# Attention values as two scaled float16 parts, and matmul operands at equal addresses modulo 512

## The chip, the cores and the metric

The kernel runs on one core of one Trainium2 chip. The metric is the device time of one execution in microseconds (us). Three runs of the kernel before gave 2252.26 us as their median (2251.11 to 2253.65).

## The reference

One layer of an encoder over 2048 frames of width 1024, all in float32. Cut to what matters here:

```python
h = rmsnorm(x, mix_norm_g)
q, k, v, u, vg = split(h @ w_in)              # 5 blocks of 512 columns; heads of 64
a = band_attention(q, k, v, q_g, k_g, rel)    # 8 heads; each 64-frame chunk sees itself and 8 before
g = spatial_gating(u, vg, norm_g, w_s, b_s)
x = x + concat(rmsnorm(a), rmsnorm(g)) @ w_out
h = rmsnorm(x, ffn_norm_g)
gate, up = split(h @ w_ffn_in)                # 2 x 2816
x = x + (silu(gate) * up) @ w_ffn_out

# in band_attention, with the probabilities of one head:
p = softmax(q @ k.T * 64 ** -0.5 + bias)
out = p @ v
```

## The kernel before

Every large product is made from operands that are split in two: `hi` is the float32 number rounded to TensorE's float32r, `lo` the rest. `split` (L80) makes them with a cast on ScalarE (L81) and a subtraction on VectorE (L82); `mm3` (L84) then runs three matmuls into one PSUM bank, hi by hi (L85), hi by lo (L86) and lo by hi (L87). Matmuls of 128 rows by 512 columns of this kind make up most of the program.

The stages, in order of time:

- **Input projection.** Two halves (`hf`) of 8 frame tiles by five column blocks (`b`: u, vg, q, k, v). `project` runs 24 matmuls for a tile of 128 frames (stationary `xh`/`xl`, moving `wh`/`wl`), and the block's `unit_*` takes the PSUM bank `ps`. There are four such banks. The next block's weights are loaded and split by `load_w` (L256), called when a block is at its seventh tile. In the first half a scheduler sets the order on every engine; from the second half on TensorE follows the order of the code. The first four tiles' attention (`early`) is woven into the second half.
- `unit_v` (L393) scales `ps` by the frame's `rx` on ScalarE and writes it as three bfloat16 parts: cast (L397), subtract (L398), cast (L399), subtract (L400), then a DMA to `v_d`.
- **Attention** of tiles 4 to 15, 96 (tile, head) steps, with the output projection's matmuls (`po`) fed between them. In each step TensorE makes the scores `S` (L171), transposes five 128x128 blocks of probabilities `pr` against the identity `ident` (L195, L198) and multiplies (`values`, L206). The transposed probabilities are two float16 parts, `ph` (cast with `PSCALE` on ScalarE, L201) and `pl` (VectorE, L202). For each of the five key blocks `values` runs five matmuls of 64 columns, `ph` with the three parts of v and `pl` with two:

```python
seq = [(i, a, c) for i in range(nk) for a, cs in ((ph, 3), (pl, 2)) for c in range(cs)]
for n, (i, a, c) in enumerate(seq):
    nc.tensor.matmul(o, lhsT=a[:, i], rhs=vt[m + 1 - nk + i][:, c, h * HD : (h + 1) * HD], ...)
```

  The four early tiles have 1, 2, 3 and 4 key blocks and run the same code into `ev`; together that is 480 and 80 key blocks. `denominators` (L212) divides by the row sums.
- **First FFN product**, by a seven-product (Strassen) scheme: 44 blocks of 7 products of 12 matmuls (`bank`, stationary `wih`/`wil`, moving `yh`/`yl`), 3696 in all.
- **Second FFN product**, the same scheme: 7 products of 264 matmuls (`bank`, stationary `ah`/`al`, moving `oh`/`ol`), 1848 in all.

Tiles are placed by pools that grow from the left and from the right end of the on-chip memory. Small first tiles (`edge` on the right; the constants `ident`, `nhalf`, `g1`, `rx`, `identr` on the left) shift everything allocated after them, so an operand's address within a partition, taken modulo 512 bytes, follows from their sizes.

Of the kernel before, what the change touches and what calls it, by code (L numbers as in the profile page):

```python
# [8 lines left out]
F32 = mybir.dt.float32  # L9
F32R = mybir.dt.float32r  # L10
F16 = mybir.dt.float16
BF16 = mybir.dt.bfloat16
AF = mybir.ActivationFunctionType
ALU = mybir.AluOpType
AX = mybir.AxisListType
# [3 lines left out]
P = 128  # L19
SEQ = 2048  # L20
D = 1024
KT = D // P
NT = SEQ // P
H = 8
HD = 64
AW = H * HD
# [6 lines left out]
EPS = 1e-6  # L33
NEG = -1e30
PSCALE = 16384.0
NE = WIN - 1
EARLY = [(m, h) for h in range(H) for m in range(NE)]
LATE = [(m, h) for m in range(NE, NT) for h in range(H)]
# [4 lines left out]
def block_kernel(ctx: ExitStack, tc: tile.TileContext, x, xT, w_in, mixg, qg, kg, bias, sgug, wsT, bsp, outg, w_out, ffng, w_fi, w_fo, out):  # L43
    nc = tc.nc

    consts = ctx.enter_context(tc.tile_pool(name="consts", bufs=1))
    edge = ctx.enter_context(tc.tile_pool(name="edge", bufs=1, side="right"))
    edge.tile([P, 24], F32, name="edge")
    dram = ctx.enter_context(tc.tile_pool(name="dram", bufs=1, space=DRAM))

    kT_d = dram.tile([P, H, SEQ], F32, name="kT_d")
    qe_d = dram.tile([HD, H, NE, 2, P], F32, name="qe_d")
    qT_d = [qe_d[:, :, m] if m < NE else dram.tile([HD, H, 2, P], F32, name=f"qT_d{m}") for m in range(NT)]
    v_d = [dram.tile([P, 3, AW], BF16, name=f"v_d{m}") for m in range(NT)]
    g_d = [dram.tile([P, AW], F32, name=f"g_d{m}") for m in range(NT)]
    a_d = [dram.tile([P, AW], F32, name=f"a_d{m}") for m in range(NT)]
    y_d = [[[dram.tile([P, 512], F32, name=f"y_d{i}_{o}_{j}") for j in range(4)] for o in range(7)] for i in range(2)]
# [5 lines left out]
    nhalf = consts.tile([P, 8], F32, name="nhalf")  # L63
    nc.gpsimd.memset(nhalf, -0.5)

    g1 = consts.tile([P, KT], F32, name="g1")
    nc.scalar.dma_start(g1, mixg)
    rx = consts.tile([P, NT], F32, name="rx")

    def pool(stack, name, bufs, side="left", space=bass.MemoryType.SB):  # L70
        return stack.enter_context(tc.tile_pool(name=name, bufs=bufs, side=side if space != PSUM else None, space=space, reuse_waits="tile"))
# [8 lines left out]
    def split(hi, lo, src):  # L80
        nc.scalar.copy(hi, src)  # L81
        nc.vector.tensor_sub(lo, src, hi.bitcast(F32))  # L82
# [9 lines left out]
    apool = {}  # L92
    bt, vt, qd, kw, pvs, sums, xm, gn, an, mh, ml, heads = ({} for _ in range(12))
# [52 lines left out]
    def load_tile(m, q=True):  # L146
        if q:
            qd[m] = apool["qd"].tile([P, H, 2, P], F32R, tag="qd", name=f"qd{m}")
            nc.sync.dma_start(qd[m][:HD].bitcast(F32), qT_d[m])
            nc.sync.dma_start(qd[m][HD:].bitcast(F32), qT_d[m])  # L150
        vt[m] = apool["vt"].tile([P, 3, AW], BF16, tag="vt", name=f"vt{m}")
        nc.sync.dma_start(vt[m], v_d[m])

    def load_bias(h):
# [50 lines left out]
    def values(m, h, o):  # L205
        nk = min(m, WIN - 1) + 1  # L206
        ph, pl = heads.pop((m, h))
        seq = [(i, a, c) for i in range(nk) for a, cs in ((ph, 3), (pl, 2)) for c in range(cs)]
        for n, (i, a, c) in enumerate(seq):
            nc.tensor.matmul(o, lhsT=a[:, i], rhs=vt[m + 1 - nk + i][:, c, h * HD : (h + 1) * HD], start=n == 0, stop=n == len(seq) - 1)  # L210

    def denominators(pool, ss, k):  # L212
        rs = pool.tile([P, k], F32, tag="rs", name="rs")
        nc.vector.tensor_scalar_mul(rs, ss, PSCALE)
        nc.vector.reciprocal(rs, rs)
        return rs

# [18 lines left out]
    with ExitStack() as st:  # L236
        st1 = st.enter_context(ExitStack())
        tqk, raw = pool(st1, "tqk", 2), pool(st1, "raw1", 4)
        stg = st1.enter_context(ExitStack())
        big, c1 = pool(stg, "big1", 1), pool(stg, "c1", 1)  # L240
        sm, tmp, ws, xs = (pool(st, n, b, "right") for n, b in (("sm1", 4), ("tmp1", 2), ("ws", 4), ("xs", 4)))
        paux = pool(st, "paux", 4, space=PSUM)
# [10 lines left out]
                nc.vector.scalar_tensor_tensor(lo[:, j], r[:, j], s, hi[:, j].bitcast(F32), op0=ALU.mult, op1=ALU.subtract)  # L253
            return hi, lo

        def load_w(b, kp):  # L256
            r = raw.tile([P, 2, 512], F32, tag="raw", name=f"wr{b}_{kp}")
            hi = ws.tile([P, 2, 512], F32R, tag="wh", name=f"wh{b}_{kp}")
            lo = ws.tile([P, 2, 512], F32R, tag="wl", name=f"wl{b}_{kp}")
            nc.sync.dma_start(r, w_in[b, :, 2 * kp : 2 * kp + 2])  # L260
            split(hi, lo, r)
            return hi, lo

        def x_stats(t):
# [7 lines left out]
        def project(xt, w, tl, between=None):  # L272
            ps = pmm.tile([P, 512], F32, tag="mm", name="ps")
            c, o = divmod(tl, 4)
            s = slice(o * P, (o + 1) * P)
            for kt in range(KT):
                kp, j = divmod(kt, 2)
                xh, xl = xt[c][kp]
                wh, wl = w[kp]
                mm3(ps, xh[:, j, s], xl[:, j, s], wh[:, j], wl[:, j], kt == 0, kt == KT - 1)  # L280
                if between and kt in (1, 4, 7):
                    between()
            return ps
# [107 lines left out]
            later(3, fin)  # L391

        def unit_v(t, ps):  # L393
            e = tmp.tile([P, AW], F32, tag="f", name="ev", bufs=5)
            nc.scalar.activation(e, ps, AF.Copy, scale=rx[:, t : t + 1])
            vp = tmp.tile([P, 3, AW], BF16, tag="vp", name="vp")
            nc.scalar.copy(vp[:, 0], e)  # L397
            nc.vector.tensor_tensor(e, e, vp[:, 0], op=ALU.subtract)  # L398
            nc.scalar.copy(vp[:, 1], e)  # L399
            nc.vector.tensor_tensor(vp[:, 2], e, vp[:, 1], op=ALU.subtract)  # L400
            nc.sync.dma_start(v_d[t], vp)


        ep, eq, ek, eb, es, ev = ({} for _ in range(6))

        def open_early(stack):
            for n, bufs in (("in", 2), ("vt", 1), ("pr", 2), ("pp", 2), ("an", 1), ("sa", 4)):
                ep[n] = pool(stack, "e" + n, bufs)
            for m in range(NE):
                vt[m] = ep["vt"].tile([P, 3, AW], BF16, name=f"vte{m}")  # L410
                nc.sync.dma_start(vt[m], v_d[m])
            ep["a"] = ep["an"].tile([P, NE, H, HD], F32, name="a4")
            for h in range(2):
                early_in(h)
# [11 lines left out]
        def early(i):  # L426
            sp = dict(S=(paux, "aux"), T=(paux, "aux"), ap=ep, w=NE * P)
            if i < len(EARLY):
                m, h = EARLY[i]
                if m == 0:  # L430
                    es[h] = ep["sa"].tile([P, NE], F32, tag="es", name="es")
                scores(m, h, sp, eq[h][:, m], ek[h], eb[h], es[h][:, m : m + 1])
            if 1 <= i <= len(EARLY):
                m, h = EARLY[i - 1]
                flip(m, h, sp)
            if 2 <= i < len(EARLY) + 2:
                m, h = EARLY[i - 2]
                if m == 0:
                    ev[h] = paux.tile([P, NE, HD], F32, tag="aux", name="ev", padded_shape=[P, 8, HD])
                values(m, h, ev[h][:, m])  # L440
                if m == NE - 1:
                    rs = denominators(ep["sa"], es[h], NE)
                    nc.vector.tensor_tensor(ep["a"][:, :, h], ev[h], rs.unsqueeze(2).to_broadcast([P, NE, HD]), op=ALU.mult)
                    if h + 2 < H:
                        early_in(h + 2)
            if i == len(EARLY) + 2:
                for m in range(NE):
                    a = ep["a"][:, m].rearrange("p h d -> p (h d)")
                    att_scale(ep, a)
                    nc.sync.dma_start(a_d[m], a)  # L450
# [37 lines left out]
        for hf in range(2):  # L488
            for b, unit in enumerate(blocks):
                for tl in range(8):  # L490
                    t = hf * 8 + tl
                    if (hf, b, tl) == (1, 4, 2):
                        while due:
                            tick()
                        st1.close()
                        open_out(st_out)
                        mx["P"] = (paux, "aux")
                    if (hf, b) == (1, 4) and tl in (6, 7):
                        an[tl - 6] = None
                        mix_g(tl - 6)  # L500
                        mix_a(tl - 6)
                    if (hf, b, tl) == (1, 0, 0):
                        st.enter_context(tc.manual_schedule(engines={mybir.EngineType.PE}))
                    if (hf, b, tl) == (1, 2, 3):
                        stg.close()
                        open_early(st1)
                    unit(t, project([xts[2 * hf], xts[2 * hf + 1]], w, tl, step if hf == 1 and b in (2, 3) and 8 * b + tl >= 20 else None))
                    tick()
                    if hf == 0 and b == 4 and tl in (3, 7):
                        c = 2 + tl // 4  # L510
                        xts[c] = [load_x(c, kp) for kp in range(4)]
                        for tt in range(4):
                            x_stats(4 * c + tt)
                    if tl == 6 and (hf, b) != (1, 4):
                        nw = [load_w((b + 1) % 5, kp) for kp in range(4)]
                w = nw


# [370 lines left out]
```

## Time and profile before

| | |
|---|---|
| median of three runs | 2252.26 us (2251.11 to 2253.65) |
| the profiled execution's own time | 2248.34 us |
| its span, first to last instruction | 2246.6 us |
| mean granted TensorE clock | 0.998 of full speed |
| busy share of the span: TensorE, VectorE, ScalarE, GpSimd | 98%, 56%, 41%, 41% |
| chain that ended last: TensorE | 82% |

A matmul's busy time in the profile is its whole passage, modelled, and matmuls overlap: what one costs on a saturated TensorE is the distance from its start to the start of the next. In a timeline row the first number is the start; in a row of windows the number behind x counts the matmuls that touch the stretch, so one or two at the edges are counted too much.

### The profile page before, as it was taken

To read this page: it belongs to the slowest core of one execution; us is meant where nothing else is said; L and a number is where in the kernel's file an instruction comes from. 1 tells how busy PE (TensorE), PEld (TensorE's weight loads), DVE (VectorE), ACT (ScalarE), POOL (GpSimd) and SP (SyncE) were. 2 spreads that over 40 slices of the span, in tenths; PEclk is the share of its full clock that TensorE was granted. 3 is DMA by queue.
4 is the path that set the end of the run, shared out by engine and by line. 5 is a ranking of instruction groups with operands and counts; after the bars stand their busy time and mean duration, and the time that the engine had idled before them with its cause. 6 is when DMAs were issued, how large, how long until landed. Compare 5 with 4: busy or idle time off the path is not lost.

```text
span 2246.6 us, 33040 instructions
## 1 busy us (share of the span) xinstructions
PE 2200.9 (98%) x12648; PEld 1810.0 (81%) x12648; DVE 1268.4 (56%) x1799; ACT 911.8 (41%) x1663; POOL 915.8 (41%) x789
## 2 busy tenths in 40 slices
PE   8999999999999999799999998999999999999999
PEld 7888888887888888688888886788888878888787
DVE  3366345774666666775555558565555533544555
ACT  6434544554555555443333335333332323222322
POOL 1254114320011100756566665665656412603434
PEclk9999999999999999999999999999999999999999
DMA  7244616558878873932323236232323263733463
GB/s 259 76 131 135 221 66 191 166 168 295 252 226 265 265 234 131 298 118 90 122 89 120 82 131 194 89 121 89 113 89 113 95 234 134 283 117 119 151 229 133
DMA packets 183805, 361.37 MB, mean 161 GB/s; under 512 B 15328, under 2 KB 68576, under 8 KB 182112
## 3 DMA queue, kind: packets, MB, share of 16 engines
q1 hardware_dynamic: 183504, 359.27, 48.0%
q8 instruction: 99, 1.62, 0.3%
q14 instruction: 58, 0.48, 0.1%
q10 hardware_dynamic: 144, 0.00, 0.0%
HBM read 256.45 MB, written 102.76 MB: 160 GB/s over the span
## 4 chain that ended last, share of the span: by engine, by line
PE 82%; DVE 4%; POOL 4%; DMA 4%; issue 3%; ACT 2%; SPq 1%; POOLq 0%; DVEq 0%; ACTq 0%
PE bank L85 17%; PE bank L86 17%; PE bank L87 17%; PE ps L85 6%; PE ps L86 6%; PE ps L87 6%; PE pv L210 2%; PE S L171 2%; PE pt L198 2%; PE po L85 2%; PE po L87 2%; PE po L86 2%; DMA kTw<-kT_d 1%; DMA ynat<-y_d 1%; POOL g L723 1%
## 5 line engine op out<-in xcount | busy, mean ns | idle before, releaser
L86 PE MATMUL bank<-yl,wih 128*128 128x512 f32 x1232 | 486.5, 395 | 4.0 <-DVE yl L82 4.0
L85 PE MATMUL bank<-yh,wih 128*128 128x512 f32 x1232 | 483.4, 395 | 7.0 <-ACT wih L81 5.0
L87 PE MATMUL bank<-yh,wil 128*128 128x512 f32 x1232 | 482.4, 394 | 0.0
L85 PEld LDWEIGHTS bank<-yh,wih 128*128 128x128 f32 x1232 | 232.2, 189 | 63.5 <-ACT wih L81 5.4
L86 PEld LDWEIGHTS bank<-yl,wih 128*128 128x128 f32 x1232 | 232.1, 188 | 60.7 <-DVE yl L82 7.1
L87 PEld LDWEIGHTS bank<-yh,wil 128*128 128x128 f32 x1232 | 232.0, 188 | 53.8
L85 PE MATMUL ps<-wh,xh 128*128 128x512 f32 x640 | 251.7, 398 | 7.9 <-ACT wh L81 7.9
L86 PE MATMUL ps<-wl,xh 128*128 128x512 f32 x640 | 250.2, 392 | 1.7 <-DVE wl L82 1.7
L87 PE MATMUL ps<-wh,xl 128*128 128x512 f32 x640 | 250.4, 391 | 0.0
L86 PE MATMUL bank<-ol,ah 128*128 128x512 f32 x616 | 243.1, 395 | 0.0
L85 PE MATMUL bank<-oh,ah 128*128 128x512 f32 x616 | 240.8, 395 | 1.0 <-ACT oh L81 1.0
L82 DVE TENSOR_TENSOR al<-ar,ah 128x1024 fp32r<-128x1024 f32 x77 | 109.5, 1421 | 212.8 <-ACT ah L81 212.7
L87 PE MATMUL bank<-oh,al 128*128 128x512 f32 x616 | 224.5, 395 | 1.7 <-DVE al L82 1.7
L82 DVE TENSOR_TENSOR wil<-s,wih 128x512 fp32r<-128x512 f32 x176 | 172.6, 1013 | 76.5 <-ACT wih L81 76.3
L81 ACT CAST ah<-ar 128x1024 fp32r<-128x1024 f32 x77 | 80.8, 1049 | 301.7 <-PE bank L86 281.2
L723 POOL TENSOR_TENSOR g<-up,g 128x512 f32<-128x512 f32 x88 | 138.6, 1576 | 82.2 <-DVE up L722 82.2
L81 ACT CAST wih<-s 128x512 fp32r<-128x512 f32 x176 | 101.5, 617 | 169.2 <-POOL s L700 116.1
L85 PEld LDWEIGHTS ps<-wh,xh 128*128 128x128 f32 x640 | 120.6, 189 | 31.0 <-ACT wh L81 7.9
L81 ACT CAST wih<-wir 128x512 fp32r<-128x512 f32 x132 | 81.5, 617 | 157.7 <-PE bank L86 144.9
L86 PEld LDWEIGHTS ps<-wl,xh 128*128 128x128 f32 x640 | 120.6, 188 | 25.9 <-DVE wl L82 2.5
L87 PEld LDWEIGHTS ps<-wh,xl 128*128 128x128 f32 x640 | 120.4, 188 | 25.0
L87 PEld LDWEIGHTS bank<-oh,al 128*128 128x128 f32 x616 | 116.0, 188 | 29.2 <-DVE al L82 2.2
(175 smaller groups left out, 4092.7 us busy)
## 6 DMA issues: line engine op xcount, KB each, us to landing
wir<-in_w_fi SPq DMA_DIRECT2D x88, 512.0 KB, 3.3
ar<-f_d SPq DMA_DIRECT2D x77, 512.0 KB, 3.3
kTw<-kT_d SPq DMA_DIRECT2D x96, 320.0 KB, 4.1
f_d<-g SPq DMA_DIRECT2D x22, 1024.0 KB, 4.2
wr<-in_w_in SPq DMA_DIRECT2D x40, 512.0 KB, 5.0
f_d<-c SPq DMA_DIRECT2D x22, 768.0 KB, 4.5
wor<-in_w_fo SPq DMA_DIRECT2D x66, 256.0 KB, 3.7
ynat<-y_d SPq DMA_DIRECT2D x56, 256.0 KB, 4.6
```

Source lines behind the costliest of these rows:

```text
L81: nc.scalar.copy(hi, src)
L82: nc.vector.tensor_sub(lo, src, hi.bitcast(F32))
L85: nc.tensor.matmul(ps, lhsT=lh, rhs=rh, start=first, stop=False)
L86: nc.tensor.matmul(ps, lhsT=lh, rhs=rl, start=False, stop=False)
L87: nc.tensor.matmul(ps, lhsT=ll, rhs=rh, start=False, stop=last)
L171: nc.tensor.matmul(S[:, i, :hw], lhsT=q[:, p], rhs=k[:, i * hw : (i + 1) * hw], start=p == 0, stop=p == 1)
L198: nc.tensor.transpose(pt[:, i], pr[:, i * P : (i + 1) * P], ident)
L210: nc.tensor.matmul(o, lhsT=a[:, i], rhs=vt[m + 1 - nk + i][:, c, h * HD : (h + 1) * HD], start=n == 0, stop=n == len(seq) - 1)
L723: nc.gpsimd.tensor_tensor(g[:, i], t, g[:, i], op=ALU.mult)
```

## The change

1. The attention values are written as two float16 parts (cast, subtract) instead of three bfloat16 parts, and `values` runs four matmuls for a key block instead of five: `ph` and `pl` with both parts.
2. So that float16's range holds them, v is multiplied per head by `vs` before it is split, and `denominators` takes `PSCALE` times `vs`. `vs` comes from a bound: `v_norms` squares the v columns of `w_in` times `g1` (ScalarE) and sums them over each head's columns (VectorE), eight times while the v weights are loaded in the first half; `v_scales` sums over the partitions with one small matmul against `ones`, one VectorE sum, two GpSimd operations and one on VectorE. `unit_v` now reads its PSUM bank on VectorE, and does so only when `vs` is there.
3. `edge` grows from 24 to 120 words and a tile `skip` of 48 words comes ahead of `ident`; with the new constants this moves the tiles. Start addresses of matmul operands in the two built programs, modulo 512 bytes:

| matmuls | number | before: stationary, moving | after |
|---|---|---|---|
| input projection `xh`/`xl`, `wh`/`wl` | 1920 | 0, 0 | 128, 128 |
| late scores `qd`, `kTw` | 384 | 128, 128 or 384 | 256, 256 or 0 |
| output projection `mh`/`ml`, `woh`/`wol` | 768 | 256, 256 | 0, 0 |
| first FFN `wih`/`wil`, `yh`/`yl` | 2640 | 384, 256 | 0, 0 |
| the same, two of the seven `yh`/`yl` pairs | 1056 | 384, 384 | 0, 0 |
| second FFN `ah`/`al`, `oh`/`ol` | 1848 | 256, 384 | 0, 0 |
| float32 transposes (`pr`, `gn`, `a`, `h`), `ident` | 816 | 384 or 256, 128 | 0 or 256, 320 |
| values `ph`/`pl`, `vt`/`vte` | 2800, after 2240 | differences 0, 128, 256, 384 | the same differences |

```diff
+VTOP = 32768.0 / D ** 0.5
...
-    edge.tile([P, 24], F32, name="edge")
+    edge.tile([P, 120], F32, name="edge")
+    consts.tile([P, 48], F32, name="skip")
...
-    v_d = [dram.tile([P, 3, AW], BF16, name=f"v_d{m}") for m in range(NT)]
+    v_d = [dram.tile([P, 2, AW], F16, name=f"v_d{m}") for m in range(NT)]
...
+    vs = consts.tile([P, H], F32, name="vs")
+    vsp = consts.tile([P, H], F32, name="vsp")
+    ones = consts.tile([P, P], F32, name="ones")
+    nc.gpsimd.memset(ones, 1.0)
...
-        seq = [(i, a, c) for i in range(nk) for a, cs in ((ph, 3), (pl, 2)) for c in range(cs)]
+        seq = [(i, a, c) for i in range(nk) for a in (ph, pl) for c in range(2)]
...
-    def denominators(pool, ss, k):
+    def denominators(pool, ss, k, h=None):
         rs = pool.tile([P, k], F32, tag="rs", name="rs")
-        nc.vector.tensor_scalar_mul(rs, ss, PSCALE)
+        if h is None:
+            nc.vector.tensor_mul(rs, ss, vsp)
+        else:
+            nc.vector.tensor_scalar_mul(rs, ss, vsp[:, h : h + 1])
         nc.vector.reciprocal(rs, rs)
...
-        def load_w(b, kp):
+        def load_w(b, kp, norms=False):
...
             split(hi, lo, r)
+            if norms:
+                v_norms(kp, r)
             return hi, lo
...
         def unit_v(t, ps):
-            e = tmp.tile([P, AW], F32, tag="f", name="ev", bufs=5)
-            nc.scalar.activation(e, ps, AF.Copy, scale=rx[:, t : t + 1])
-            vp = tmp.tile([P, 3, AW], BF16, tag="vp", name="vp")
+            e = tmp.tile([P, H, HD], F32, tag="f", name="ev", bufs=5)
+            nc.vector.scalar_tensor_tensor(e, ps.rearrange("p (h d) -> p h d", h=H), rx[:, t : t + 1], vs.unsqueeze(2).to_broadcast([P, H, HD]), op0=ALU.mult, op1=ALU.mult)
+            e = e.rearrange("p h d -> p (h d)")
+            vp = tmp.tile([P, 2, AW], F16, tag="vp", name="vp")
             nc.scalar.copy(vp[:, 0], e)
-            nc.vector.tensor_tensor(e, e, vp[:, 0], op=ALU.subtract)
-            nc.scalar.copy(vp[:, 1], e)
-            nc.vector.tensor_tensor(vp[:, 2], e, vp[:, 1], op=ALU.subtract)
+            nc.vector.tensor_tensor(vp[:, 1], e, vp[:, 0], op=ALU.subtract)
             nc.sync.dma_start(v_d[t], vp)
+
+
+        vq = {}
+
+        def v_norms(kp, r):
+            if kp == 0:
+                vq["sq"] = tqk.tile([P, H, KT], F32, name="vq", bufs=1)
+            for j in range(2):
+                k = 2 * kp + j
+                q = tmp.tile([P, H, HD], F32, tag="f", name="wq", bufs=5)
+                nc.scalar.activation(q, r[:, j].rearrange("p (h d) -> p h d", h=H), AF.Square, scale=g1[:, k : k + 1])
+                nc.vector.tensor_reduce(vq["sq"][:, :, k], q, axis=AX.X, op=ALU.add)
+
+        def v_scales():
+            pn = paux.tile([P, H, KT], F32, tag="aux", name="pn", padded_shape=[P, H, HD])
+            nc.tensor.matmul(pn, lhsT=ones, rhs=vq["sq"], start=True, stop=True)
+            ss = sm.tile([P, H], F32, tag="ssh", name="vss")
+            nc.vector.tensor_reduce(ss, pn, axis=AX.X, op=ALU.add)
+            ms = sm.tile([P, H], F32, tag="rhm", name="vsm")
+            nc.gpsimd.tensor_scalar(ms, ss, VTOP ** -2, 1e-30, op0=ALU.mult, op1=ALU.add)
+            nc.gpsimd.tensor_tensor(vs, ms, nhalf, op=ALU.pow)
+            nc.vector.tensor_scalar_mul(vsp, vs, PSCALE)
...
-                    rs = denominators(ep["sa"], es[h], NE)
+                    rs = denominators(ep["sa"], es[h], NE, h)
...
+                    if (hf, b, tl) == (0, 4, 0):
+                        v_scales()
...
-                        nw = [load_w((b + 1) % 5, kp) for kp in range(4)]
+                        nw = [load_w((b + 1) % 5, kp, (hf, b) == (0, 3)) for kp in range(4)]
```

The other lines of the diff give `vt` and `vte` the shape `[P, 2, AW]` in float16.

TensorE, a key block of `values` in the first step of the late attention (`pv_...` is the PSUM bank, `vt_...` a value tile). Before:

```order
L210 LDWEIGHTS ph
L210 MATMUL pv_5852<-vt_5587,ph 128x64
L210 LDWEIGHTS ph
L210 MATMUL pv_5852<-vt_5587,ph 128x64
L210 LDWEIGHTS ph
L210 MATMUL pv_5852<-vt_5587,ph 128x64
L210 LDWEIGHTS pl
L210 MATMUL pv_5852<-vt_5587,pl 128x64
L210 LDWEIGHTS pl
L210 MATMUL pv_5852<-vt_5587,pl 128x64
```

Now:

```order
L216 LDWEIGHTS ph
L216 MATMUL pv_5778<-vt_5513,ph 128x64
L216 LDWEIGHTS ph
L216 MATMUL pv_5778<-vt_5513,ph 128x64
L216 LDWEIGHTS pl
L216 MATMUL pv_5778<-vt_5513,pl 128x64
L216 LDWEIGHTS pl
L216 MATMUL pv_5778<-vt_5513,pl 128x64
```

One matmul with `ph` is gone, and its weight load with it.

VectorE where the v weights of the first half are split (`wl_0` to `wl_3`, between the k block's last tiles). Before:

```order
L82 TENSOR_TENSOR wl_0_1952<-wr_0_1950,wh_0_1951 128x1024
L82 TENSOR_TENSOR wl_1_1958<-wr_1_1956,wh_1_1957 128x1024
L348 TENSOR_TENSOR e<-e,rhr 128x512
L82 TENSOR_TENSOR wl_2_1964<-wr_2_1962,wh_2_1963 128x1024
L388 CAST kT<-ptk 128x512
L374 TENSOR_TENSOR e<-e,gk 128x512
L82 TENSOR_TENSOR wl_3_1970<-wr_3_1968,wh_3_1969 128x1024
```

Now:

```order
L88 TENSOR_TENSOR wl_0_1957<-wr_0_1955,wh_0_1956 128x1024
L423 TENSOR_REDUCE vq<-wq 128x8
L359 TENSOR_TENSOR e<-e,rhr 128x512
L88 TENSOR_TENSOR wl_1_1970<-wr_1_1968,wh_1_1969 128x1024
L423 TENSOR_REDUCE vq<-wq 128x8
L399 CAST kT<-ptk 128x512
L385 TENSOR_TENSOR e<-e,gk 128x512
L88 TENSOR_TENSOR wl_2_1982<-wr_2_1980,wh_2_1981 128x1024
L423 TENSOR_REDUCE vq<-wq 128x8 x2
L88 TENSOR_TENSOR wl_3_1994<-wr_3_1992,wh_3_1993 128x1024
L423 TENSOR_REDUCE vq<-wq 128x8
```

Five of the eight sums stand between and behind the splits; the other three stand a few rows earlier.

TensorE where the small matmul stands, in the v block of the first half (only in the kernel after the change):

```order
L92 MATMUL ps<-wl_3_1994,xh_3_300 128x512
L93 MATMUL ps<-wh_3_1993,xl_3_301 128x512
L91 MATMUL ps<-wh_3_1993,xh_3_300 128x512
L427 MATMUL pn<-vq,ones 128x8x8
L92 MATMUL ps<-wl_3_1994,xh_3_300 128x512
L93 MATMUL ps<-wh_3_1993,xl_3_301 128x512
L395 MATMUL ptk<-identr,kc 128x128 x8
```

58 projection matmuls of the block and 8 transposes stand ahead of it; 38 more projection matmuls and 16 transposes stand between it and the first matmul of the block's fifth tile, which needs a PSUM bank that `unit_v` has emptied.

## Rows read from the trace of the kernel before

**Rows 1.** The page: TensorE's busy time, and its granted clock in 40 slices.
```profile
PE 2200.9 (98%) x12648; PEld 1810.0 (81%) x12648; DVE 1268.4 (56%) x1799; ACT 911.8 (41%) x1663; POOL 915.8 (41%) x789
...
PEclk9999999999999999999999999999999999999999
```
**Rows 2.** Windows: length, busy time by engine, granted clock, DMA share, GB/s.
```profile
364.00:470.00 106.00, 102.95 (x899) 88.82 (x899) 72.08 (x175) 55.81 (x136) 35.44 (x44) 1.00 0.53 148
542.00:898.00 356.00, 351.61 (x4055) 301.79 (x4054) 234.53 (x493) 198.07 (x479) 39.57 (x74) 1.00 0.75 235
960.00:1380.00 420.00, 420.00 (x1815) 340.24 (x1814) 247.44 (x302) 148.24 (x248) 259.60 (x178) 1.00 0.33 113
...
1803.00:2246.00 443.00, 436.04 (x1875) 352.66 (x1873) 214.22 (x205) 126.34 (x166) 158.13 (x102) 1.00 0.49 174
```
**Rows 3.** Timeline of TensorE, a step of the late attention: start, length, instruction.
```profile
702.50 0.26 PE L210 MATMUL pv<-vt,ph 128*128 128x64 bf16 x3
702.60 0.22 PE L210 MATMUL pv<-vt,pl 128*128 128x64 bf16 x2
...
703.18 0.22 PE L210 MATMUL pv<-vt,pl 128*128 128x64 bf16 x2
703.24 0.83 PE L171 MATMUL S<-kTw,qd 128*128 128x320 f32 x4
...
705.87 0.26 PE L210 MATMUL pv<-vt,ph 128*128 128x64 bf16 x3
```
**Rows 4.** Timeline of VectorE, the same step.
```profile
703.31 0.68 DVE L202 SCALAR_TENSOR_TENSOR pl<-pt,ph 128x512 f16<-128x512 f32 x1
```
**Rows 5.** Timeline of TensorE, first FFN product.
```profile
1060.20 0.39 PE L85 MATMUL bank<-yh,wih 128*128 128x512 f32 x1
...
1073.49 0.39 PE L85 MATMUL bank<-yh,wih 128*128 128x512 f32 x1
...
1076.23 0.39 PE L85 MATMUL bank<-yh,wih 128*128 128x512 f32 x1
```
**Rows 6.** Windows, TensorE alone: input projection, first FFN, second FFN.
```profile
53.09:80.29 27.20, 27.20 (x121) 1.00 0.21 72
1059.96:1254.50 194.54, 194.54 (x842) 1.00 0.29 103
1860.13:2083.22 223.09, 223.09 (x962) 1.00 0.47 164
```
**Rows 7.** Groups by line: count, busy us, mean ns of one, idle before.
```profile
L395 ACT ACTIVATE ev<-ps,rx 128x512 f32<-128x512 f32 x16 | 10.9, 682 | 18.1 <-PE ps L87 18.0
L399 ACT CAST vp<-ev 128x512 bf16<-128x512 f32 x16 | 9.9, 616 | 7.6 <-DVE ev L398 7.6
L317 ACT ACTIVATE jv<-vf 128x512 bf16<-128x512 f32 x16 | 10.1, 630 | 0.7
L346 DVE TENSOR_REDUCE ssh<-sq 128x8 f32<-128x512 f32 x32 | 21.7, 678 | 4.3 <-POOL sq L344 4.3
L77 POOL TENSOR_TENSOR rhr<-rhm,nhalf 128x8 f32<-128x8 f32 x32 | 54.8, 1713 | 2.5
```
**Rows 8.** Timeline of VectorE where the v weights are split.
```profile
198.21 2.37 DVE L82 TENSOR_TENSOR wl<-wr,wh 128x1024 fp32r<-128x1024 f32 x2
...
201.58 1.22 DVE L82 TENSOR_TENSOR wl<-wr,wh 128x1024 fp32r<-128x1024 f32 x1
...
204.17 1.21 DVE L82 TENSOR_TENSOR wl<-wr,wh 128x1024 fp32r<-128x1024 f32 x1
```
**Rows 9.** Timeline of TensorE, transposes of a late step.
```profile
701.36 0.60 PE L198 MATMUL pt<-ident,pr 128*128 128x128 f32 x4
701.72 0.48 PE L85 MATMUL po<-woh,mh 128*128 128x512 f32 x1
```
**Rows 10.** Timeline of TensorE, gating matmuls of 256 columns.
```profile
83.49 0.28 PE L86 MATMUL pm<-vl,wsh 128*128 128x256 f32 x1
...
84.44 0.40 PE L85 MATMUL ps<-wh,xh 128*128 128x512 f32 x1
```

More of the change, by code (lines that the diff above doesn't have):

```diff
@@ L150, in load_tile @@
             nc.sync.dma_start(qd[m][HD:].bitcast(F32), qT_d[m])
-        vt[m] = apool["vt"].tile([P, 3, AW], BF16, tag="vt", name=f"vt{m}")
+        vt[m] = apool["vt"].tile([P, 2, AW], F16, tag="vt", name=f"vt{m}")
         nc.sync.dma_start(vt[m], v_d[m])
@@ L409, in open_early @@
             for m in range(NE):
-                vt[m] = ep["vt"].tile([P, 3, AW], BF16, name=f"vte{m}")
+                vt[m] = ep["vt"].tile([P, 2, AW], F16, name=f"vte{m}")
                 nc.sync.dma_start(vt[m], v_d[m])
```

## The prediction

> **What bounds the kernel now.** I read the page first: TensorE is busy for 98% of the span, the other engines for 41 to 56%, and its clock is granted in full (2.4 GHz) in every slice [rows 1]. A busy matmul is a modelled passage, so this alone proves little. The windows by stage come next: from 960 to 1380 us TensorE has no idle time at all, in the late attention it idles for 4.4 of 356 us, in the early attention for 3.1 of 106, in the second FFN product for 7 of 443, while none of VectorE, ScalarE and GpSimd is busy for more than 68% of any of these stretches [rows 2]. So the end is set by how closely matmuls follow one another, and a term is worth the number of matmuls times the distance from start to start. That distance is what I looked for in the timelines.
>
> **Values.** A late step's 25 matmuls of 64 columns run from 702.50 to 703.24 us, where the scores follow without a gap [rows 3]: 0.74 us, 29.6 ns each, although each has its own weight load. The change takes 5 of the 25 away, with their loads: 0.148 us in each of 96 steps, **14.2 us**. The early tiles have 80 key blocks, so 80 x 29.6 ns = **2.4 us**. Would another engine then be late? In this step VectorE writes `pl` from 703.31, for 0.68 us [rows 4], and the values that read it start at 705.87 [rows 3]; that is 1.9 us of slack against 0.15 us taken out. I therefore count the late gain whole. The early gain lies between nothing (that stage's 3.1 us of waits grow by it) and 2.4; I take 2.4, since its TensorE is 97% busy.
>
> **Equal addresses.** The first FFN product holds its own experiment. Five of its seven products have operands 128 bytes apart modulo 512 and two have equal ones. From 1060.20 to 1073.49 us stand 57 starts of the first kind, 13.29 us or 233.2 ns each; from 1073.49 to 1076.23 the 12 matmuls of a product of the second kind, 228.3 ns each [rows 5]. The mix checks: 5/7 x 233.2 + 2/7 x 228.3 = 231.8, and 840 matmuls took 194.54 us, 231.6 each [rows 6]. The second FFN product, all at a difference of 384, takes 223.09 us for 960 matmuls, 232.4 each, and the input projection, all at equal addresses, 27.20 us for 120, 226.7 each [rows 6]. Same engine, same clock, same shape: what sorts them is the difference. After the change all 5544 FFN matmuls have equal addresses. I price those that change at the 228.3 ns of the same stage, and keep 226.7 as the other bound:
>
> - first FFN: 2640 x (233.2 - 228.3) = **12.9 us** (17.2 at 226.7);
> - second FFN: 1848 x (232.4 - 228.3) = **7.6 us** (10.5 at 226.7).
>
> The input and output projections and the scores keep their differences, so they change by nothing. The Trainium skill speaks against this term. "TensorE: Matmul & The Clock Gate", section "Step-by-step: what each phase is for", says that TensorE reads the stationary and the moving operand through two independent ports, so that loading the next weights takes nothing from the running matmul. By it addresses could not matter and this term would be zero. The rows above disagree with it by 4 to 6 ns per matmul.
>
> **Transposes.** The 816 float32 transposes go from differences of 128 or 256 to 192 or 448, which no row shows for them. They stand about 90 ns apart now (four from 701.36 to 701.72 us [rows 9]). The nearest row for an odd difference (32 or 288) is the gating product's: eight matmuls of 256 columns in 0.95 us [rows 10], 119 ns each, 12 above the 106.7 of 256 columns at 2.4 GHz, where the 512-column matmuls lie 13 to 20 above their 213.3. Nothing is out of line there. I take zero, with 5 ns either way as bounds (the step between the two kinds above): 4 us up or down.
>
> **Making the scales.** ScalarE gets eight squares, about 630 ns each (the nearest row is a square of the same size), 5.0 us, and VectorE eight sums at 678 ns, 5.4 us [rows 7]. VectorE is nearly full there: its splits of the v weights run from 198.21 to 205.38 us with other work between [rows 8]. With five sums in and behind them the last split moves by up to 2.7 us (four sums ahead of it), if the other three sums fit in earlier. TensorE meanwhile has work on three tiles for each slice of weights (18 matmuls, 4.1 us), so I expect it to find each slice ready. The small matmul waits for the last sum, and everything on TensorE queues behind it; that is one sum, 0.7 us, past the last split. The chain behind it is a sum (0.7), GpSimd's power (1.7, with a short operation before it) and two on VectorE, about 3.5 us, beside 38 matmuls of 227 ns and 16 transposes, some 10 us, before a fifth bank is needed. So the cost lies between 0 and 5.4 + 3.5 = 8.9 us, with every sum and the whole chain uncovered; it is nearer to none, as the cover is longer than each piece. I take **1 us**. A gain is excluded, since TensorE has no idle time there to give back.
>
> **The rest costs nothing.** `unit_v` loses the scaling copy and the second cast on ScalarE (682 + 616 ns for each of 16 tiles [rows 7]) and trades one VectorE operation for another; both engines' idle time covers it, and TensorE does not feel it. If `unit_v` fell behind, four PSUM banks would cover one tile of 24 matmuls. DMAs for v shrink by a third. `denominators` has the same number of operations.
>
> **Sum.** 14.2 + 2.4 + 12.9 + 7.6 - 1 = 36.1 us less. The profiled execution took 2248.3 us, which gives 2212.2; the median of the runs shown lies 3.9 above the profiled one, so the forecast for the median is **2216 us**.
>
> **Rivals.**
>
> 1. *Addresses do nothing*: the 5 ns would come from where in a block the slow products stand. For it: the equal pairs always belong to the last two of the seven products. Against it: the input projection and the second FFN, with other neighbours, fall on the same sides [rows 6]. Only the values' term is left: 16.6 - 1, so 2236.7 us. The two ports of the Trainium skill's page above would have it so.
> 2. *The attention is held by the chain of VectorE and ScalarE*, and the shorter steps turn into waits for `pl` or the probabilities. For it: VectorE is busy for 234.5 of 356 us there [rows 2]. Against it: the 1.9 us of slack. Then 12.9 + 7.6 - 1 = 19.5 us, so 2232.8.
> 3. *The transposes become slower* (the other side). `ident` moves to a difference of 192, and each transpose has its own weight load beside it. It decides when 816 transposes cost 36.1 us more, 44 ns each; if they doubled from 90 ns, 73 us, the end would be 2252.3 - 36.1 + 73.4 = 2290 us. Against it: no difference in these rows is worth more than some 6 ns, and the gating rows show none of it.
>
> **Chances and range.** Forecast 82%, rival 1 8%, rival 2 7%, rival 3 3%. Below the forecast the bounds are 226.7 ns for the 4488 matmuls (7 us) and the transposes (4 us): both together give 2205. Above it lie the scales (7.9 us more than taken) and the transposes (4 us), and rival 2 at 2232.8; so 2205 to 2233, which leaves rivals 1 and 3 out. Measurements of this kernel tell 0.2%, 4.5 us, from no change. All but rival 3 are faster by far more: 0.96 faster; rival 3 gives slower 0.03, and 0.01 for a case between.
>
> **What would show it.** Right: values rows of four matmuls a key block, 20 in about 0.59 us; both FFN products at about 228 ns from start to start in every product; transposes still near 90 ns; no wait of TensorE over 2 us around the small matmul near 200 us. Wrong: FFN products that keep 233 and 232 ns (rival 1); new waits for `pl` or the probabilities in the late attention (rival 2); transposes over 100 ns (rival 3); or a wait for `vq` or the v weights of several us.

## The result, and the profile after

| | before | after |
|---|---|---|
| median | 2252.22 us, 4 runs (2251.11 to 2253.65) | 2213.43 us, 4 runs (2210.12 to 2215.7) |
| the profiled execution's own time, span | 2248.34, 2246.6 us | 2214.4, 2212.6 us |
| mean granted TensorE clock in it | 0.998 | 0.994 |

The ratio is 0.9826, with a 95% interval of 0.9809 to 0.9843: 38.8 us less from median to median, where 36.1 had been forecast. The profiled execution of after lies 1 us above its median, that of before 3.9 below its own; between the two profiled ones the difference is 33.9 us.

The page of after, against [rows 1]. TensorE has 558 matmuls fewer (560 values gone, one small matmul that the trace shows as two) and stays at 98%:

```profile
PE 2162.9 (98%) x12090; PEld 1796.8 (81%) x12090; DVE 1275.4 (58%) x1809; ACT 899.7 (41%) x1639; POOL 912.4 (41%) x792
...
PEclk9999999999999999999999999999999999999999
```

The time by stages: I cut both traces where a stage's first matmul starts. Windows of before at these cuts: the first block of the input projection, the late attention, the second FFN product (length; PE, PEld, DVE, ACT, POOL busy; granted clock, DMA share, GB/s):

```profile
7.90:53.10 45.20, 45.20 (x193) 37.31 (x194) 18.36 (x23) 30.74 (x45) 6.44 (x17) 1.00 0.77 260
...
542.40:889.00 346.60, 342.32 (x3943) 294.20 (x3942) 230.25 (x482) 195.04 (x472) 39.57 (x74) 1.00 0.77 241
...
1803.40:2241.80 438.40, 435.63 (x1873) 352.35 (x1871) 213.13 (x203) 126.34 (x166) 158.13 (x102) 1.00 0.49 173
```

The same stages of after, with the early attention between (against the second line of [rows 2]):

```profile
8.10:54.00 45.90, 45.90 (x193) 37.76 (x194) 18.30 (x23) 30.71 (x45) 6.47 (x17) 1.00 0.76 255
364.00:476.00 112.00, 105.49 (x826) 89.91 (x825) 73.78 (x178) 57.91 (x139) 35.78 (x44) 0.97 0.51 144
548.40:877.80 329.40, 327.01 (x3478) 280.19 (x3477) 225.80 (x482) 197.61 (x472) 39.77 (x73) 1.00 0.79 246
...
1778.50:2208.40 429.90, 426.52 (x1873) 352.07 (x1871) 213.56 (x203) 126.58 (x166) 157.46 (x102) 1.00 0.51 176
```

The late attention is 17.2 us shorter, the second FFN product 8.4. The first FFN product runs from 929.05 to 1803.4 us before and from 919.4 to 1778.4 after: 15.4 shorter. The first row is 0.7 longer (TensorE's granted clock came up to 2.4 GHz at 12.95 us, not at 11.30). The early row has 6.5 us without a matmul and a granted clock of 0.97; this is the stage that lost most. In the whole, from the first projection block that carries early work (335.1 us before, 336.8 after) to the projection's end (523.5 and 529.55), before took 188.4 us and after 192.75: 4.4 us *more*, where 2.4 less had been forecast.

A late step, TensorE's timeline of after, against [rows 3, 9]. Twenty values from 700.08 to 700.67 us, 0.59 us or 29.6 ns each, then the scores at once; four transposes from 702.13 to 702.49, as far apart as before:

```profile
700.08 0.23 PE L216 MATMUL pv<-vt,ph 128*128 128x64 f16 x2
...
700.61 0.22 PE L216 MATMUL pv<-vt,pl 128*128 128x64 f16 x2
700.67 0.82 PE L177 MATMUL S<-kTw,qd 128*128 128x320 f32 x4
...
702.13 0.60 PE L204 MATMUL pt<-ident,pr 128*128 128x128 f32 x4
702.49 0.47 PE L91 MATMUL po<-woh,mh 128*128 128x512 f32 x1
```

Windows of TensorE alone, 150 us of the first FFN product and 200 of the second (length, PE busy, matmuls that touch it, clock, DMA share, GB/s). Before:

```profile
1100.00:1250.00 150.00, 150.00 (x649) 1.00 0.28 102
...
1850.00:2050.00 200.00, 200.00 (x863) 1.00 0.47 165
```

After, in the same windows:

```profile
1100.00:1250.00 150.00, 150.00 (x663) 1.00 0.30 106
...
1850.00:2050.00 200.00, 200.00 (x884) 1.00 0.50 172
```

Two touch the edges; 200 us over some 882 starts are 226.8 ns each, over 861 they are 232.3. Over all starts of a stage at full clock and without a wait, the means are 226.81 ns in the first product of after (233.04 and, for its two equal products, 228.0 before) and 226.69 in the second (232.38 before). These whole-stage means are used below; the windows show the same by count.

**Where the early attention lost.** GpSimd's timeline of before, in the q block of the second half. `rhr` is what the normalization of a tile's q waits for, all eight heads at once. The memset (`be`, L424) writes a corner of the early bias and waits for the DMA that fills the rest of the tile; it stands behind `rhr`, so its wait holds nobody:

```profile
366.41 0.20 POOL L75 TENSOR_SCALAR rhm<-ssh 128x8 f32<-128x8 f32 x1 [0.81 <-DVE ssh L346]
366.69 1.64 POOL L77 TENSOR_TENSOR rhr<-rhm,nhalf 128x8 f32<-128x8 f32 x1
369.56 0.14 POOL L424 MEMSET be<- 64x64 f32 x1 [1.23 <-DMA be<-in_bias]
```

GpSimd's timeline of after. The scheduler put the second memset ahead, and `rhm` and `rhr` wait for a DMA that they don't need:

```profile
370.54 0.14 POOL L456 MEMSET be<- 64x64 f32 x1 [3.06 <-DMA be<-in_bias]
370.77 0.20 POOL L81 TENSOR_SCALAR rhm<-ssh 128x8 f32<-128x8 f32 x1
371.05 1.64 POOL L83 TENSOR_TENSOR rhr<-rhm,nhalf 128x8 f32<-128x8 f32 x1
```

What follows from it, VectorE's and TensorE's timeline of after. VectorE idles for 3.45 us, and q's transposes on TensorE stand for 3.59:

```profile
372.72 0.69 DVE L359 TENSOR_TENSOR e<-e,rhr 128x512 f32<-128x512 f32 x1 [3.45 <-POOL rhr L83]
...
375.32 0.75 PE L372 MATMUL ptq<-identr,qs 128*128 128x128 f32 x4 [3.59 <-DVE nmx L186]
375.87 0.76 PE L91 MATMUL ps<-wh,xh 128*128 128x512 f32 x1
376.42 0.63 PE L92 MATMUL ps<-wl,xh 128*128 128x512 f32 x1
```

The last rows show a second price: most matmuls stand 0.43 us apart, the first of them 0.55, not 0.23. Windows of TensorE alone in after, at every stretch at half clock (1.2 GHz) between start and end:

```profile
374.80:381.60 6.80, 6.28 (x26) 0.50 0.47 113
893.60:897.00 3.40, 3.40 (x11) 0.50 0.41 161
938.00:941.40 3.40, 3.22 (x9) 0.50 1.05 345
1378.30:1385.10 6.80, 5.50 (x13) 0.50 0.20 60
2095.10:2098.50 3.40, 3.40 (x10) 0.50 0.79 236
```

Before has two such stretches, 6.8 us from 946.6 and 3.4 from 1397.1: 10.2 us together, against 23.8. At half speed a projection or FFN matmul stands 0.43 us from the next in these stretches, nearly twice the 0.23 of full speed, so close to half of the difference, up to 6.8 us, is time that after lost and before did not. Up to 3.4 of it comes with the wait at 371. The rest is in part chance: before's profiled execution has a mean clock of 0.998, its runs beside the experiments 0.995 to 0.998. At the end of the late attention TensorE waits 2.1 to 2.3 us for `xm` in all eleven traces of this document, and half speed follows in three of them (after, `val_only`, `corner`), not in `after_again`, which is the same program as after.

**Making the scales**, timelines of VectorE, TensorE, GpSimd and VectorE of after, against [rows 8]. The last split starts at 208.49 us, the last sum at 209.62; the small matmul comes 5 us later and the scaled values 2.8 us after that, with no wait of TensorE over 0.5 us from 196 to 218 us:

```profile
208.49 1.22 DVE L88 TENSOR_TENSOR wl<-wr,wh 128x1024 fp32r<-128x1024 f32 x1
209.62 0.68 DVE L423 TENSOR_REDUCE vq<-wq 128x8 f32<-128x512 f32 x1
...
214.79 0.33 PE L427 MATMUL pn<-vq,ones 128*128 128x64 f32 x2
...
215.75 1.64 POOL L432 TENSOR_TENSOR vs<-vsm,nhalf 128x8 f32<-128x8 f32 x1
...
217.59 1.40 DVE L406 SCALAR_TENSOR_TENSOR ev<-ps,rx,vs 128x512 f32<-128x512 f32 x2
```

### The profile page after: what moved, and what is told of

Its sections match the earlier page's. It is cut to its first block, busy times and chain, and to the rows that moved or that the text cites. A ratio compares the mean times of both kernels' runs of the same rounds, so it can differ in the third digit from the quotient of the medians.

```text
span 2212.6 us, 31917 instructions
## 1 busy us (share of the span) xinstructions
PE 2162.9 (98%) x12090; PEld 1796.8 (81%) x12090; DVE 1275.4 (58%) x1809; ACT 899.7 (41%) x1639; POOL 912.4 (41%) x792
## 4 chain that ended last, share of the span: by engine, by line
PE 71%; issue 11%; POOL 6%; DVE 6%; DMA 3%; ACT 1%; SPq 1%; DVEq 0%; POOLq 0%; ACTq 0%
PE bank L91 16%; PE bank L93 16%; PE bank L92 16%; PE ps L91 5%; PE ps L92 5%; PE ps L93 5%; DVE wil L88 1%; PE S L177 1%; PE pt L204 1%; PE po L91 1%; PE po L93 1%; PE po L92 1%; POOL g L757 1%; PE pv L216 1%; POOL rhr L83 1%
## 5 line engine op out<-in xcount | busy, mean ns | idle before, releaser
L92 PE MATMUL bank<-yl,wih 128*128 128x512 f32 x1232 | 481.3, 391 | 5.8 <-DVE yl L88 5.8
L91 PE MATMUL bank<-yh,wih 128*128 128x512 f32 x1232 | 478.3, 391 | 8.6 <-ACT wih L87 3.8
L93 PE MATMUL bank<-yh,wil 128*128 128x512 f32 x1232 | 477.2, 390 | 0.0
L92 PEld LDWEIGHTS bank<-yl,wih 128*128 128x128 f32 x1232 | 232.3, 189 | 57.0 <-DVE yl L88 8.8
L88 DVE TENSOR_TENSOR wil<-s,wih 128x512 fp32r<-128x512 f32 x176 | 178.4, 1051 | 89.3 <-ACT wih L87 89.1
L733 POOL TENSOR_TENSOR s<-wir 128x512 f32<-128x512 f32 x44 | 58.7, 1334 | 194.3 <-DMA wir<-in_w_fi 181.1
```

The source lines that it names most:

```text
L91: nc.tensor.matmul(ps, lhsT=lh, rhs=rh, start=first, stop=False)
L92: nc.tensor.matmul(ps, lhsT=lh, rhs=rl, start=False, stop=False)
L93: nc.tensor.matmul(ps, lhsT=ll, rhs=rh, start=False, stop=last)
L733: nc.gpsimd.tensor_add(s1, x21, x22)
```

## The experiments

Distances from start to start are means over all matmuls of a stage. A difference of addresses is the stationary operand's start minus the moving one's, modulo 512. The first five kernels were timed in rounds, each against the kernel before on its own chip; the four `dist` kernels ran once, and only their distances decide.

### The kernel after once more

> The changed kernel once more, as the measure for the two runs beside it. Expected 2208 to 2216 us, median near 2213. In its trace the same 3.6 us wait of TensorE for the second group of q transposes near 371 us, with GpSimd's memset of the second bias corner (waiting for its DMA) ahead of the power operation, and the clock at half speed for some microseconds behind that wait in most executions. If the wait is a chance of one execution (rival), it is not there again.

2211.66 us (2209.47 to 2212.52), ratio 0.9823 (0.9810 to 0.9837), beside a before of 2251.0. The wait at 371 is here too, with half speed behind it. This run is the yardstick for `val_only`, `no_norms` and `corner`, which ran beside it; `addr_only` ran on another chip, beside a before of its own.

### Either half alone

The values' half, with before's addresses put back (a change to after):

```diff
-    edge.tile([P, 120], F32, name="edge")
-    consts.tile([P, 48], F32, name="skip")
+    edge.tile([P, 24], F32, name="edge")
+    consts.tile([P, 112], F32, name="skip")
```

> The changed kernel with the addresses of before: edge of 24 words and a skip of 112, so that operands stand 128 and 384 bytes apart again in the FFN products. Theory: FFN matmuls follow at 233 ns (first product, 5 of 7), 228 (the equal pairs) and 232 (second product) as before the change; only the values' part is left, 14.2 us in the late attention and 2.4 in the early one, less about 1 for the scales and about 6 for the wait near 371 us with its clock: 2252 - 10 = 2242 us, 2236 to 2246. Rival 1 (addresses do nothing): the FFN products stay at 227 ns and the time at 2213. Rival 2 (the attention is held by VectorE and ScalarE): 2250 and over.

2238.51 us (2237.26 to 2239.26), ratio 0.9944 (0.9930 to 0.9957): 12.5 us less than before. Its FFN products stand where before's do: 233.00 ns at 128, 228.08 for the equal pairs, 232.38 at 384.

The addresses' half, with before's values (a change to before):

```diff
-    edge.tile([P, 24], F32, name="edge")
+    edge.tile([P, 120], F32, name="edge")
+    consts.tile([P, 192], F32, name="skip")
```

> The kernel before with the addresses of the change alone: edge of 120 words, skip of 192, three bfloat16 parts and five matmuls a key block as before. Theory: all FFN matmuls at 226.7 ns from start to start; 2640 x 6.3 + 1056 x 1.2 + 1848 x 5.7 ns = 28 us less, some of it lost to waits: 2226 us, 2222 to 2230. No long wait near 371 us, as GpSimd's order is that of before. Rival (addresses do nothing, the gain comes from something else in the change): 2252.

2225.48 us (2224.15 to 2226.48), ratio 0.9887 (0.9871 to 0.9904), beside a before of 2252.04: 26.6 us less, from tiles that hold nothing. The first FFN product stands at 226.78 ns, the second at 226.70. The windows of the two products, as above:

```profile
1100.00:1250.00 150.00, 150.00 (x664) 1.00 0.29 106
...
1850.00:2050.00 200.00, 200.00 (x884) 1.00 0.47 167
```

That is the addresses' effect shown by itself, and rival 1 is out. The two halves, each against the before of its own chip, add up: 12.5 + 26.6 = 39.1, against 39.3 for `after_again`.

The waits of TensorE for q's transposes (total, times, longest) sort the loss at 371. The addresses' half:

```profile
PE ptq L362 <- DVE nmx L181: 1.7, 2, 1.1
```

The values' half:

```profile
PE ptq L372 <- DVE nmx L186: 4.8, 2, 3.8
```

So the long wait comes with the values' edit. The other traces agree: all eight that have the new values and after's memset (after, `after_again`, `val_only`, `no_norms` and the four `dist` kernels) show a wait of 3.3 to 4.0 us there and half speed with it; before and `addr_only` show neither.

### Without the scales

A change to after: no norms and no `v_scales`, `vs` is the constant 1024. This leaves out the bound from the weights.

```diff
+    nc.gpsimd.memset(vs, 1024.0)
+    nc.gpsimd.memset(vsp, 1024.0 * PSCALE)
...
-                    if (hf, b, tl) == (0, 4, 0):
-                        v_scales()
...
-                        nw = [load_w((b + 1) % 5, kp, (hf, b) == (0, 3)) for kp in range(4)]
+                        nw = [load_w((b + 1) % 5, kp) for kp in range(4)]
```

> The changed kernel without the weight norms: no squares, no sums, no small matmul; the scales are a constant 1024, set at the start. It leaves out the bound that fits the scale to the weights. Theory: making the scales costs about 1 us in the first half's v block and nothing else; the median is 0.5 to 1.5 us under the changed kernel's of the same chip and the wait near 371 us stays. Rival: the norms are also behind the wait near 371 us, or cost TensorE more than the stage shows; then the median is 5 to 9 us lower.

2210.34 us (2208.53 to 2212.23), ratio 0.9819 (0.9805 to 0.9832): 1.3 us under `after_again`, with ranges that overlap. Making the scales costs at most a microsecond or two, and isn't told from nothing here. The 4.0 us wait for `ptq` stays, so the norms didn't cause it:

```profile
PE ptq L374 <- DVE nmx L188: 5.1, 2, 4.0
```

### The memset off the DMA

A change to after in `early_in`: the corner is written first, and the bias comes by two DMAs that leave the corner out, so that the memset has no DMA to wait for.

```diff
-            nc.sync.dma_start(eb[h], bias[h][:, BANDW - NE * P :])
             nc.gpsimd.memset(eb[h][:CHUNK, NE * P - CHUNK :], NEG)
+            nc.sync.dma_start(eb[h][CHUNK:], bias[h][CHUNK:, BANDW - NE * P :])
+            nc.sync.dma_start(eb[h][:CHUNK, : NE * P - CHUNK], bias[h][:CHUNK, BANDW - NE * P : BANDW - CHUNK])
```

> The changed kernel, with the corner of the early bias tiles set before the DMA and the DMA split in two that leave the corner out, so that GpSimd's memset waits for no transfer. Theory: the 3.6 us wait near 371 us in the changed kernel, and the 3.4 us that 6.8 us of half clock behind it cost, come from GpSimd waiting for the bias DMA with the power operation queued behind; without it TensorE waits there for about 1.2 us as before the change, and the median is 4 to 6 us under the changed kernel's of the same chip, near 2208. Rival: TensorE waits there for the VectorE and ScalarE chain itself, whatever GpSimd does; then the wait stays over 3 us and the median within 1.5 us of the changed kernel's.

2203.23 us (2201.84 to 2205.25), ratio 0.9788 (0.9775 to 0.9801): 8.4 us under `after_again`, more than expected, and **under the ranges of both kernels**. On GpSimd `rhm` now waits for `ssh` alone:

```profile
366.63 0.20 POOL L81 TENSOR_SCALAR rhm<-ssh 128x8 f32<-128x8 f32 x1 [1.45 <-DVE ssh L357]
```

The early attention of this kernel, in the window and the units of the stages above:

```profile
364.00:476.00 112.00, 110.15 (x865) 1.00 0.54 151
```

Its waits for q's transposes:

```profile
PE ptq L372 <- DVE nmx L186: 0.6, 1, 0.6
```

From the block at 337.2 us to the projection's end it takes 183.6 us, `after_again` 192.7. Of these 9.1 us, 4.5 are the waits (5.1 against 0.6) and 3.4 the clock: `after_again` ran at half speed for 3.4 us from 376.6 and again from 407.3, this kernel, after its start, nowhere before 885. Some 1.2 us are in smaller waits or not traced. The edit gives more than it was meant to, since it also takes away the wait of the first memset, which stood ahead of `sq` for 4.1 us in before and 4.3 in after. That may be why q's transposes wait less here (0.6 us) than in before (2.2); it was not tried by itself. So the loss at 371, and the half clock behind it, are shown to come from the memset's wait for its DMA. Why the scheduler puts that memset ahead of `rhm` once the values are written another way was not tried.

### How far apart the operands may start

Four changes of one number in after, each of which moves only what lies on the right side:

```diff
-    edge.tile([P, 120], F32, name="edge")
+    edge.tile([P, 112], F32, name="edge")    (dist32)
+    edge.tile([P, 104], F32, name="edge")    (dist64)
+    edge.tile([P, 56], F32, name="edge")     (dist256)
+    edge.tile([P, 8], F32, name="edge")      (dist448)
```

They put 5 of the first FFN product's 7 products at the named difference and the second FFN product at 512 less it; the two equal products of the first stay equal.

> The changed kernel with edge 8 words smaller, so that operands of five of the seven first FFN products stand 32 bytes apart modulo 512, those of the second FFN product 480, and two first FFN products stay equal. Theory A (only equal addresses are quick): about 232 to 233 ns from start to start where the addresses differ, 227 to 228 where they are equal; about 2236 us. Theory B (what counts is the overlap of the two reads, so a small distance does little): 227 to 229 everywhere, 2213 to 2218 us.

> As the run at 32 bytes, with edge 16 words smaller: 64 bytes apart in five first FFN products, 448 in the second FFN product. Theory A: 232 to 233 ns where they differ, about 2236 us. Theory B: between equal and 128 apart, 228 to 231 ns.

> As the run at 32 bytes, with edge 64 words smaller: 256 bytes apart in five first FFN products and in the second FFN product. Theory A (the cycle is 512 bytes): 232 to 233 ns or more, about 2237 us. Theory C (the cycle is 256 bytes or less, and equal modulo that is enough, as the late scores at 256 suggest, which were no slower): 227 ns everywhere, about 2213 us.

> The kernel after with `edge` 112 words shorter: 2640 matmuls of the first FFN product have their stationary operand 448 bytes ahead of the moving one (modulo 512), all 1848 of the second one 64. With the two the other way round (64 and 448) the first stood 233.3 ns from start to start and the second 228.9. Theory S, the side counts: what is dear is a stationary operand that starts 64 bytes behind the moving one, whatever the product. Then the first product stands near 229 ns and the second near 233.3; against the kernel after that is 2640 x 2.2 + 1848 x 6.6 = 18 us more, near 2231. Theory T, the stage counts and not the side: the first product stays near 233.3 ns and the second near 228.9, so 2640 x 6.5 + 1848 x 2.2 = 21 us more, near 2234. The sums lie too close to tell them apart; the windows of the two products do. If both stood at 226.8 (2213), only 64 in the first product would be dear, and neither holds.

| kernel | time, us | first FFN: difference, ns | second FFN: difference, ns |
|---|---|---|---|
| after | 2211.66 to 2213.43 | 0: 226.81 | 0: 226.69 |
| dist32 | 2240.04 | 32: 233.40 | 480: 233.32 |
| dist64 | 2230.73 | 64: 233.33 | 448: 228.90 |
| before | 2252.22 | 128: 233.04 | 384: 232.38 |
| dist256 | 2211.97 | 256: 226.76 | 256: 226.69 |
| dist448 | 2231.93 | 448: 229.48 | 64: 233.33 |

The windows of the two stages, as above. `dist64`:

```profile
1100.00:1250.00 150.00, 150.00 (x649) 1.00 0.27 96
...
1850.00:2050.00 200.00, 200.00 (x875) 1.00 0.47 167
```

`dist448`, the same differences with the stages exchanged:

```profile
1100.00:1250.00 150.00, 150.00 (x657) 1.00 0.28 99
...
1850.00:2050.00 200.00, 200.00 (x859) 1.00 0.46 163
```

`dist256`:

```profile
1100.00:1250.00 150.00, 150.00 (x664) 1.00 0.29 106
...
1850.00:2050.00 200.00, 200.00 (x884) 1.00 0.49 172
```

At 256 both products are as quick as at 0: to be equal modulo 256 is enough, as theory C had it. It is the relation that counts, not the place: the input projection's two operands start at equal addresses in every kernel, but at other ones (0 in before, 128 in after, 160 in `dist32`, 192 in `dist64`, 384 in `dist256`, 64 in `dist448`), and 120 starts of its second block take 27.2 us in each. `dist32` keeps the full price on both sides (32 and 480), so a small distance is no help. `dist64` fits no theory as it was written: one product at the full price, the other at a third of it. `dist448` settles which of the two reasons holds. The count of the second product falls from 875 to 859 and that of the first rises from 649 to 657: at this distance the price goes with the side, not the stage. (In its expectation the word "behind" should read "ahead": the numbers there belong to a stationary operand 64 bytes ahead of the moving one, and that is the dear side.) With it 64 ahead a matmul stands at 233.3 ns, with it 64 behind at 228.9 to 229.5. Differences of 128 and 384 are the same modulo 256 and cost nearly the same (233.0 and 232.4). Why a difference costs anything, and why one side of 64 costs less when both of 32 are dear, stays open.

## Why the prediction was right

The sum was right to 3 us (36.1 against 38.8 between the medians and 33.9 between the profiled executions), and the mechanism in both main terms, but the closeness is partly luck, by cancellation: one term had the wrong sign, and three were too small.

- **The late values** (14.2 us): the 20 rows of a step take 0.59 us, as forecast, so 14.2 is shown by count. The stage gave 17.2. TensorE's idle time in it fell from 4.3 to 2.4 us, for 1.9 of the remaining 3; among the waits gone is one of 1.3 us of the scores for VectorE's `h`. Part of the last 1.1 us comes with the addresses: without its waits, the stretch from the first late scores to the last late values takes 350.4 us in before, 349.7 in `addr_only`, 335.8 in `val_only` and 334.6 in after. The slack of 1.9 us at [rows 4] held: the stage shows no new wait.
- **The early values** (2.4 us): this step failed. "I take 2.4, since its TensorE is 97% busy" looked at TensorE and not at what was queued ahead of `rhr` on GpSimd. The stage lost 4.4: 2.4 saved, some 3.5 of waits and up to 3.4 of half clock added. The lower bound, nothing gained, was wrong too: a reordered stage can lose. In the corner kernel the term is there: 183.6 us against before's 188.4, 2.1 of it in waits that before has and that kernel has not, 2.7 left.
- **First FFN** (12.9, or 17.2 at 226.7): 15.4. The other bound was the right price. I took the 228.3 ns of the equal products as that of equal addresses in this stage; but they stood among unequal neighbours: in before the first three of an equal product's twelve starts stand at 231.6 ns on the mean, those from the fourth on at 226.8. With all equal, all come to 226.8. By count 2640 x (233.04 - 226.81) + 1056 x (228.0 - 226.81) = 17.7 us; longer waits for `yl`, `wih` and the activations (14.4 against 11.1 us) gave 3.3 back, a shorter one of the transposes for `h` (2.9 against 4.6) added 1.7, and 0.7 is not traced.
- **Second FFN** (7.6, or 10.5): 8.4. By count 1848 x (232.38 - 226.69) = 10.5; up to 1.7 was lost at half clock from 2095, 0.6 in waits.
- **The scales** (1 us): 0.8 in this trace, from the shift of the block behind (336.8 against 335.1) less the 0.9 with which after's first block ended late. The same stretch is only 0.2 us longer than before's in `after_again` and 0.1 in `corner`, so the scales cost between nothing and 0.8. The last split starts at 208.49 us against 204.17 [rows 8], of which 0.7 was there when the weights were called; that is more than the 2.7 allowed, but TensorE's one wait from 196 to 218 us is of 0.26 us.
- **Transposes** (0): in the late attention a transpose into `pt` and the next start are 88.0 ns apart (372 of 384; the other 12 stand 165 ns apart), 88.2 before; all transposes at full clock and without a wait come to 99.6, 99.7 before. **The rest** (0): no wait of TensorE for `unit_v` shows. The stretch between late attention and first FFN product grew by 1.5, most of it the half clock at 893.6, which belongs to the execution and not to the change.

Together: 0.9 + 0.8 + 4.4 - 17.2 + 1.5 - 15.4 - 8.4 = -33.4, with 0.5 at the tail the 33.9 by which the span fell.

The rivals. Rival 1 is refuted by `addr_only`. The Trainium skill's page "TensorE: Matmul & The Clock Gate", section "Step-by-step: what each phase is for", has the loading of weights take nothing from the running matmul. No run here times a load apart from its matmul; what they show is that the pair costs 226.8 ns at one relation of addresses and 233.3 at another, which a rule without addresses doesn't tell apart. Rival 2 had the attention held by VectorE and ScalarE; the late one isn't. What went wrong in the early one is near to it, a chain behind TensorE, but its cause was GpSimd's order and a DMA. Rival 3 is out by the 88.0 ns of the transposes.

## What to carry to other kernels

On a saturated TensorE, compare start-to-start distances of equal matmuls by the addresses of their two operands: 6 ns on each of 4488 matmuls was worth 26.6 us and cost one unused tile on either side. When one edit changes what a scheduler orders, read every in-order queue for instructions that wait on a DMA and now stand ahead of a chain that TensorE waits for; here a memset of a corner, issued ahead of DMAs that leave the corner out, gave 8.4 us. And price such a wait with the half-speed stretch behind it: here 3.6 us of waiting brought up to 3.4 more.

## What was not expected of the hardware

- Operand starts that are equal modulo 256 bytes are enough: 226.7 to 226.8 ns at differences of 0 and 256, 232.4 to 233.4 at 32, 64, 128, 384 and 480.
- The side counts at 64 bytes: 233.3 ns with the stationary operand ahead, 228.9 to 229.5 with it behind. At 32 bytes it doesn't: 233.4 and 233.3.
- A product pays for its neighbours: equal products between unequal ones stand at 228.0 to 228.4 ns, between equal ones at 226.8. In before it is the first three starts of the twelve that pay (231.6).
- The granted clock of after falls to half in five short stretches. The first begins in a 3.59 us wait, one at 893.6 lies behind a wait of 2.15 us, one at 938.0 lies behind a wait of 2.87 us for `h`. The four runs of after stand in the order of their mean clocks: 0.993, 0.994, 0.995 and 0.996 with 2215.7, 2214.4, 2212.5 and 2210.1 us.
